# Weight sums made once during the input projection, activation sums on VectorE, and a deeper fetch in a hybrid encoder layer

## The chip, the cores and the metric

The kernel runs on one core of a Trainium2 chip. A core has five engines with a queue of instructions each: TensorE (PE in the profile; its weight loads are PEld), VectorE (DVE), ScalarE (ACT), GpSimd (POOL), and SyncE (SP), which here does nothing but issue transfers. Sixteen DMA engines move data between the chip's main memory and the on-chip buffers. An engine works through its own queue in order and waits where an operand or a buffer is not ready, so one waiting instruction holds up everything behind it on that engine. The metric is the device time of one execution in microseconds (us); lower is better.

## The reference, cut to what matters

One layer is computed for two groups of requests: a prompt of 2048 tokens and 8 x 16 tokens of samples with caches. Both share the weights.

```
h   = RMSNorm(x)
z   = h @ w_in                               # (tokens, 1024) @ (1024, 3592)
A   = chunk-band attention of z's q, k, v    # 8 heads x 64, own chunk + 8 before
B   = mLSTM matrix memory of z's q, k, v, o  # 4 heads x 128
x   = x + RMSNorm(concat(RMSNorm(A), sigmoid(o) * RMSNorm(B)) @ w_out)
u   = RMSNorm(x) @ w_up                      # (tokens, 1024) @ (1024, 5632)
y   = causal depthwise conv of width 3 over u's tokens, plus a bias
gate, up = halves of y's columns
x   = x + RMSNorm((gelu(gate) * up) @ w_down)   # (tokens, 2816) @ (2816, 1024)
```

Everything is float32. The change touches how w_up and w_down, and the activations gelu(gate) * up, are prepared for their two products.

## The kernel before, in words

**Precision.** A float32 matrix is split into a rounded part and the rest (a copy on ScalarE, a subtraction on VectorE: `split`, L1293 to L1295), and each product is made of three matmuls (`mm3`, L97 to L101).

**Two stages.** The first (to about 1340 us) makes the input projection, attention, the mLSTM and the output projection. The loop over `seq` (L1252 onwards) goes through 14 groups of projection columns for each of two halves of the tokens. A group yields after every few matmuls (12 steps for the groups qk and qb; 18 or 16, in the first or second half, for va and vo), and at each step `pump` lets attention and mLSTM work run beside it. Attention work is read back from main memory: the projections are stored there by transfers on ScalarE's queue and loaded by SP's.

The second stage is the feed-forward network, in three blocks of tokens (`FBLOCKS`: 768, 768 and the rest). Each block makes 22 feature tiles of the up-projection and then the down-projection.

**Seven products instead of eight.** The up-projection of every block, and the down-projection of the first two, use a Strassen-type scheme: both matrices are cut into 2 x 2 parts, sums of parts are formed, and 7 products replace 8. This needs

- four sums of the parts of w_up per feature tile. In block 0, `load_quads` (L1299) loads the four parts of a tile (128x512 each), makes the sums on VectorE (L1311), and stores them in main memory (`wsd`, L1313) for the later blocks. Three of the seven operands of the tile are kept on the chip (`raws`) for its second half. Blocks 1 and 2 load all seven from main memory.
- four sums of the parts of w_down per pair of rows. `fold_down` (L1161) makes them in the first stage on GpSimd, from 22 pieces of 512 KB in a buffer tag ("xr") that other work shares, and stores them in `wtd`. Each step of groups 1 to 12 of the first half calls it once.
- four sums of the activations per pair of feature tiles. `store_a` (L1547) stores the plain parts, forms the sums on GpSimd in place (L1559 to L1562), and stores those. Two of the sums overwrite a part that was just handed to a store, and so wait for that store.

**The down-projection** reads these activations back in pieces numbered i, of two feature tiles each: `fetch_a` (L1517) loads a piece, `split_a` (L1532) splits it. Pieces 0 and 1 go to small buffers ("q", 12 of 128x512 floats, which the weights and other work use too); later ones go to row buffers ("yq", 6 of 128x1024 floats), which the convolution's outputs y and g use as well. Pieces 2 and 3 are fetched at the first step of the down loop, later ones four ahead.

**Order.** The engines' orders are laid out when the program is built, by a planner that simulates the time of each instruction and issues what is ready. It can move an instruction ahead of others on its queue; `tc.keep_in_program_order` holds one behind the instruction that the program wrote before it on that queue.

Of the kernel before, what the change touches and what calls it, by code (L numbers as in the profile page):

```python
# [17 lines left out]
P = 128  # L18
D = 1024
# [21 lines left out]
NK = NF // 2  # L41
FORDER = [f for k in range(NK) for f in (k, k + NK)]
# [6 lines left out]
def hymba_step(ctx: ExitStack, tc: tile.TileContext, I: dict, O: dict):  # L49
# [1111 lines left out]
    def fold_down():  # L1161

        for k in range(NK):
            for c in range(2):
                cols = slice(c * 256, (c + 1) * 256)
                t = rows_tile("xr", [P, D], f"fold{k}_{c}").rearrange("p (a n) -> p a n", a=4)
                nc.sync.dma_start(t, I["w_down"][k].rearrange("p (a n) -> p a n", a=4)[:, :, cols])
                yield 0.0, 0.0
                yield 0.0, 0.0
                b11, b12, b22, b21 = [t[:, i] for i in range(4)]  # L1170
                nc.gpsimd.tensor_tensor(b11, b12, b11, op=ALU.subtract)
                nc.gpsimd.tensor_tensor(b12, b22, b12, op=ALU.subtract)
                nc.gpsimd.tensor_tensor(b22, b22, b11, op=ALU.subtract)
                nc.gpsimd.tensor_tensor(b21, b21, b22, op=ALU.subtract)
                yield 0.0, 0.0
                yield 0.0, 0.0
                nc.sync.dma_start(wtd[k].rearrange("p (a n) -> p a n", a=4)[:, :, cols], t)
                yield 0.0, 0.0
# [43 lines left out]
    folds = fold_down()  # L1222
# [5 lines left out]
    for n_, (half, gi) in enumerate(seq):  # L1228
# [68 lines left out]
    raws = {}  # L1297

    def load_quads(b, f, g):  # L1299

        src = lambda i: I["w_up"][f][:, i * 512:(i + 1) * 512]
        if b == 0 and g == 0:
            q = []
            for i in range(4):
                q.append(quad(f"wu{f}_{i}"))
                nc.sync.dma_start(q[i], src(i))
            a11, a12, a22, a21 = q
            s1, s2, s3, s4 = [quad(f"ws{f}_{i}") for i in range(4)]
            for o, x, y, op in ((s1, a21, a22, ALU.add), (s2, s1, a11, ALU.subtract), (s3, a11, a21, ALU.subtract),
                                (s4, a12, s2, ALU.subtract)):  # L1310
                nc.vector.tensor_tensor(o, x, y, op=op)  # L1311
# [12 lines left out]
        return out  # L1324
# [117 lines left out]
    for b, tiles in enumerate(FBLOCKS):  # L1442
# [74 lines left out]
        def fetch_a(i):  # L1517
# [6 lines left out]
            if i < 2:  # L1524
                g[i] = [quad(f"ar{b}_{i}_{x}")[:, :384] for x in range(2)]
                for x, r in enumerate(g[i]):
                    nc.sync.dma_start(r, src[:, 2 * c + x, :])
            else:
                g[i] = row(f"ar{b}_{i}")[:, :n_]
                nc.sync.dma_start(g[i], src[:, ks, :].rearrange("p k n -> p (k n)"))  # L1530
# [16 lines left out]
        def store_a(f, gt):  # L1547
# [11 lines left out]
            nc.gpsimd.tensor_tensor(a11, a11, a21, op=ALU.subtract)  # L1559
            nc.gpsimd.tensor_tensor(a21, a21, a22, op=ALU.add)  # L1560
            nc.gpsimd.tensor_tensor(a22, a22, a11, op=ALU.subtract)
            nc.gpsimd.tensor_tensor(a12, a12, a22, op=ALU.subtract)  # L1562
# [3 lines left out]
        for fi, f in enumerate(FORDER):  # L1566
# [23 lines left out]
            if fi == NF - 1:  # L1590
# [31 lines left out]
        if not last:  # L1622
# [47 lines left out]
            for p, (_, _, set_, onto) in enumerate(SEQUENCE):  # L1670
                for c in range(3):
# [202 lines left out]
```

## Time and profile before

| | us |
|---|---|
| median of 3 runs | 2834.72 |
| lowest and highest | 2833.73, 2836.35 |
| the profiled execution | 2845.43 |
| its span, first to last instruction | 2843.6 |
| TensorE busy in the span | 2707.8 |
| VectorE busy | 1942.6 |
| ScalarE busy | 1442.3 |
| GpSimd busy | 628.5 |

| stretch, us | what runs |
|---|---|
| 0 to 1340 | input projection, attention, mLSTM, output projection |
| 1357 to 1722 | up-projection of block 0 |
| 1711 to about 1870 | down-projection of block 0 |
| 1900 to 2200 | within the up-projection of block 1 |
| 2230 to 2406 | down-projection of block 1 |
| 2406 to 2682 | up-projection of block 2, then its down-projection to the end |

Busy times are of one profiled execution. Matmuls are pipelined and their ends modelled, so a TensorE that is busy all the time can still differ in matmuls per us; a few matmul records may be missing. The granted clock (PEclk) is 1.00 when TensorE may run at full speed. In a row of waits, the first engine and line waited, the second released it. A group's row ends with the idle time of its engine just before the group's instructions, and what ended it.

### The profile page before, as it was taken

To read this page: it belongs to the slowest core of one execution; us is meant where nothing else is said; L and a number is where in the kernel's file an instruction comes from. 1 tells how busy PE (TensorE), PEld (TensorE's weight loads), DVE (VectorE), ACT (ScalarE), POOL (GpSimd) and SP (SyncE) were. 2 spreads that over 40 slices of the span, in tenths; PEclk is the share of its full clock that TensorE was granted. 3 is DMA by queue.
4 is the path that set the end of the run, shared out by engine and by line. 5 is a ranking of instruction groups with operands and counts; after the bars stand their busy time and mean duration, and the time that the engine had idled before them with its cause. 6 is when DMAs were issued, how large, how long until landed. Compare 5 with 4: busy or idle time off the path is not lost. (4 is left out here: it accounts for less than half of the span.)

```text
span 2843.6 us, 47569 instructions
## 1 busy us (share of the span) xinstructions
PE 2707.8 (95%) x16389; PEld 2526.5 (89%) x16389; DVE 1942.6 (68%) x3503; ACT 1442.3 (51%) x2916; POOL 628.5 (22%) x1071
## 2 busy tenths in 40 slices
PE   6889999999899999999999997999999899999998
PEld 6789999988799998878889996889999778999877
DVE  4344445655545668766898997757887785888855
ACT  4244545644445666534444445655554565555543
POOL 3231000111100002244332332112232331122220
PEclk9999999999999999999999999999999999999999
DMA  7775446456564556445655556675555696655585
GB/s 233 205 225 181 130 124 184 153 167 184 167 194 127 157 156 191 126 150 188 222 177 170 173 180 217 217 238 163 175 172 159 235 336 222 195 177 168 182 318 188
DMA packets 359025, 535.12 MB, mean 188 GB/s; under 512 B 58787, under 2 KB 196479, under 8 KB 358655
## 3 DMA queue, kind: packets, MB, share of 16 engines
q1 hardware_dynamic: 318270, 491.95, 55.3%
q10 hardware_dynamic: 38592, 33.83, 3.6%
q0 software_dynamic: 1920, 6.29, 0.6%
q8 instruction: 129, 2.11, 0.3%
q14 instruction: 114, 0.93, 0.1%
HBM read 383.87 MB, written 151.21 MB: 188 GB/s over the span
## 5 line engine op out<-in xcount | busy, mean ns | idle before, releaser
L99 PE MATMUL uec<-B,wuh 128*128 128x384 f32 (+1 forms) x720 | 236.5, 330 | 4.7 <-DVE x L1584 1.8
L100 PE MATMUL uec<-B,wuh 128*128 128x384 f32 (+1 forms) x720 | 235.7, 327 | 0.0
L101 PE MATMUL uec<-B,wul 128*128 128x384 f32 (+1 forms) x720 | 234.5, 327 | 0.0
L1294 ACT CAST wuh<-wu 128x512 fp32r<-128x512 f32 x255 | 141.6, 618 | 80.6 <-PE uec L100 75.5
L1295 DVE TENSOR_TENSOR wul<-wu,wuh 128x512 fp32r<-128x512 f32 x255 | 167.5, 695 | 14.5 <-ACT wuh L1294 10.9
L99 PE MATMUL vo<-wi_h,hT 128*128 128x256 f32 x544 | 155.1, 285 | 0.6 <-DVE mt L206 0.6
L101 PE MATMUL vo<-wi_h,hT 128*128 128x256 f32 x544 | 155.6, 286 | 0.0
L100 PE MATMUL vo<-wi_l,hT 128*128 128x256 f32 x544 | 154.8, 285 | 0.0
L400 DVE CUSTOM_DVE_ANT_0 tmp<-s,nb 128x640 f32<-128x640 f32 (+4 forms) x128 | 94.3, 737 | 84.5 <-PE s L390 83.8
L1295 DVE TENSOR_TENSOR wdl<-wdr,wdh 128x512 fp32r<-128x512 f32 x198 | 130.2, 703 | 28.1 <-ACT wdh L1294 25.7
L99 PE MATMUL dn<-wdh,ah 128*128 128x512 f32 x308 | 123.3, 400 | 22.1 <-ACT ah L1294 21.1
L99 PEld LDWEIGHTS uec<-B,wuh 128*128 128x128 f32 x720 | 135.5, 188 | 9.5 <-DVE x L1584 3.1
L99 PE MATMUL qk<-hT,wi_h 128*128 128x384 f32 (+1 forms) x384 | 130.4, 340 | 7.6 <-ACT qk_st L233 4.6
L100 PEld LDWEIGHTS uec<-B,wuh 128*128 128x128 f32 x720 | 135.7, 188 | 0.2
L101 PEld LDWEIGHTS uec<-B,wul 128*128 128x128 f32 x720 | 135.5, 188 | 0.0
L1294 ACT CAST wdh<-wdr 128x512 fp32r<-128x512 f32 x198 | 111.7, 618 | 46.8 <-DMA wdr<-in_w_down 18.7
L413 DVE TENSOR_TENSOR ptl<-pt,pth 128x640 fp32r<-128x640 f32 (+4 forms) x128 | 93.6, 738 | 59.7 <-ACT pth L412 58.8
L401 ACT ACTIVATE tmp<-tmp,mn 128x640 f32<-128x640 f32 (+4 forms) x128 | 97.5, 762 | 67.5 <-DVE mn L400 61.6
L100 PE MATMUL qk<-hT,wi_h 128*128 128x384 f32 (+1 forms) x384 | 129.2, 337 | 0.0
L101 PE MATMUL qk<-hT,wi_l 128*128 128x384 f32 (+1 forms) x384 | 128.7, 335 | 0.0
L100 PE MATMUL qb<-hT,wi_h 128*128 128x384 f32 (+1 forms) x384 | 127.9, 333 | 0.0
L101 PE MATMUL dn<-wdh,al 128*128 128x512 f32 x308 | 124.5, 404 | 2.8 <-DVE al L1295 2.7
(448 smaller groups left out, 9267.0 us busy)
## 6 DMA issues: line engine op xcount, KB each, us to landing
wu<-in_w_up SPq DMA_DIRECT2D x220, 256.0 KB, 3.9
wu<-wsd SPq DMA_DIRECT2D x176, 256.0 KB, 3.8
wdr<-in_w_down SPq DMA_DIRECT2D x110, 256.0 KB, 5.5
wi_raw<-in_w_in SPq DMA_DIRECT2D x52, 512.0 KB, 4.1
wsd<-ws SPq DMA_DIRECT2D x88, 256.0 KB, 3.5
wdr<-wtd SPq DMA_DIRECT2D x88, 256.0 KB, 6.1
ad_S<-g SPq DMA_DIRECT2D x88, 192.0 KB, 1.8
ar<-ad_S SPq DMA_DIRECT2D x40, 384.0 KB, 6.3
```

The source lines that it names most:

```text
L99: nc.tensor.matmul(out, ah, bh, start=start, stop=False, skip_group_check=onto)
L100: nc.tensor.matmul(out, ah, bl, start=False, stop=False, skip_group_check=onto)
L101: nc.tensor.matmul(out, al, bh, start=False, stop=stop, skip_group_check=onto)
L400: nc.vector.tensor_tensor_reduce(o_, s_, b_, 1.0, 3e38, ALU.add, ALU.min, accum_out=mn)
L401: nc.scalar.activation(tmp[:, :n], tmp[:, :n], AF.Exp, bias=mn, scale=-1.0, accum_out=rsum[:, i % 4, hh:hh + 1])
L413: nc.vector.tensor_tensor(s.ptl[:, sl, qc], ptv, s.pth[:, sl, qc], op=ALU.subtract)
L1294: nc.scalar.copy(h, r)
L1295: nc.vector.tensor_tensor(l, r, h, op=ALU.subtract)
```

## The change

1. `folds` replaces `fold_down`. It goes through 44 pieces of w_up (22 feature tiles, two column halves) and then 22 of w_down. Each piece is 512 KB, loaded to one of three buffers of its own ("fold"), summed in place by four VectorE operations of 128x256, and stored (`wsd` or `wtd`). Loads and stores are held in program order on SP's queue. A piece is begun every 4 steps; its sums are written 3 steps and its store 5 steps after its load. The steps are those of groups 2 to 12 of both halves; what is left is done at the last group.
2. `load_quads` makes no sums any more: block 0 loads seven operands per tile from main memory like the other blocks. The places of the sums within `wsd` change with the order in which they are now made.
3. `store_a` forms the activation sums on VectorE.
4. `fetch_a` uses small buffers for pieces 0 to 4 (before: 0 and 1). Pieces 2 to 4 are fetched while the last feature tile of the block runs, after the splits of pieces 0 and 1; in the down loop the fetch of piece i + 4 begins at i = 1.

```diff
+FOLD_STEPS = 4
...
-    def fold_down():
-        for k in range(NK):
-            for c in range(2):
-                cols = slice(c * 256, (c + 1) * 256)
-                t = rows_tile("xr", [P, D], f"fold{k}_{c}").rearrange("p (a n) -> p a n", a=4)
-                nc.sync.dma_start(t, I["w_down"][k].rearrange("p (a n) -> p a n", a=4)[:, :, cols])
-                yield 0.0, 0.0
-                yield 0.0, 0.0
-                b11, b12, b22, b21 = [t[:, i] for i in range(4)]
-                nc.gpsimd.tensor_tensor(b11, b12, b11, op=ALU.subtract)
...
-                nc.sync.dma_start(wtd[k].rearrange("p (a n) -> p a n", a=4)[:, :, cols], t)
-                yield 0.0, 0.0
+    def fold_pieces():
+        for f in FORDER:
+            for c in range(2):
+                yield f"u{f}_{c}", I["w_up"][f], wsd[f], c, False
+        for k in range(NK):
+            for c in range(2):
+                yield f"d{k}_{c}", I["w_down"][k], wtd[k], c, True
+
+    def folds():
+        v4 = lambda t: t.rearrange("p (a n) -> p a n", a=4)
+        live = deque()
+        pieces = list(fold_pieces())
+
+        def load(nm, src, dst, c, down):
+            cols = slice(c * 256, (c + 1) * 256)
+            t = v4(pr.tile([P, D], F32, tag="fold", name=f"fold{nm}", bufs=3))
+            tc.keep_in_program_order(nc.sync.dma_start(t, v4(src)[:, :, cols]))
+            live.append((t, v4(dst)[:, :, cols], down))
+
+        def combine(t, dst, down):
+            a, b, c, d = [t[:, i] for i in range(4)]
+            sub = lambda o, x, y: nc.vector.tensor_tensor(o, x, y, op=ALU.subtract)
+            if down:
+                sub(a, b, a)
+                sub(b, c, b)
+                sub(c, c, a)
+                sub(d, d, c)
+            else:
+                sub(a, a, d)
+                nc.vector.tensor_tensor(d, d, c, op=ALU.add)
+                sub(c, c, a)
+                sub(b, b, c)
+
+        for n in range(FOLD_STEPS * (len(pieces) + 1)):
+            i, r = divmod(n, FOLD_STEPS)
+            if r == 0 and i < len(pieces):
+                load(*pieces[i])
+            if (n - 3) % FOLD_STEPS == 0 and 0 <= n - 3 < FOLD_STEPS * len(pieces):
+                combine(*live[-1])
+            if (n - 5) % FOLD_STEPS == 0 and 0 <= n - 5 < FOLD_STEPS * len(pieces):
+                t, dst, _ = live.popleft()
+                tc.keep_in_program_order(nc.sync.dma_start(dst, t))
+            yield
...
-            if half == 0 and 1 <= gi <= 12:
-                next(folds, None)
+            if 2 <= gi <= 12:
+                next(fold, None)
...
+        if n_ == len(seq) - 1:
+            for _ in fold:
+                pass
...
     def load_quads(b, f, g):
-        if b == 0 and g == 0:
-            q = []
-            for i in range(4):
-                q.append(quad(f"wu{f}_{i}"))
-                nc.sync.dma_start(q[i], src(i))
-            a11, a12, a22, a21 = q
-            s1, s2, s3, s4 = [quad(f"ws{f}_{i}") for i in range(4)]
-            for o, x, y, op in ((s1, a21, a22, ALU.add), (s2, s1, a11, ALU.subtract), (s3, a11, a21, ALU.subtract),
-                                (s4, a12, s2, ALU.subtract)):
-                nc.vector.tensor_tensor(o, x, y, op=op)
-            for i, o in enumerate((s2, s3, s1, s4)):
-                nc.sync.dma_start(wsd[f][:, i * 512:(i + 1) * 512], o)
-            raws[f] = [a12, a22, s4]
-            return [a11, s2, s3, s1]
-        if b == 0:
-            return raws.pop(f)
-        for i, s_ in enumerate([[src(0), kept(0), kept(1), kept(2)], [src(1), src(2), kept(3)]][g]):
+        for i, s_ in enumerate([[src(0), kept(2), kept(0), kept(3)], [src(1), src(2), kept(1)]][g]):
...
-            if i < 2:
+            if i < 5:
                 g[i] = [quad(f"ar{b}_{i}_{x}")[:, :384] for x in range(2)]
...
-            nc.gpsimd.tensor_tensor(a11, a11, a21, op=ALU.subtract)
+            nc.vector.tensor_tensor(a11, a11, a21, op=ALU.subtract)
...
                 else:
                     split_a(0)
                     split_a(1)
+                    for i in range(2, 5):
+                        fetch_a(i)
...
                         if k % 2 == 0:
-                            if i == 0:
-                                fetch_a(2)
-                                fetch_a(3)
                             if i >= 1:
                                 split_a(i + 1)
-                            fetch_a(i + 4)
+                                fetch_a(i + 4)
```

More of the change, by code (lines that the diff above doesn't have):

```diff
@@ L1159, in late_B @@
             nc.vector.tensor_tensor(lo, lo.bitcast(F32), hi, op=ALU.subtract)
-    def fold_down():
+    def fold_pieces():
+        for f in FORDER:
+            for c in range(2):
+                yield f"u{f}_{c}", I["w_up"][f], wsd[f], c, False
         for k in range(NK):
             for c in range(2):
-                cols = slice(c * 256, (c + 1) * 256)
-                t = rows_tile("xr", [P, D], f"fold{k}_{c}").rearrange("p (a n) -> p a n", a=4)
-                nc.sync.dma_start(t, I["w_down"][k].rearrange("p (a n) -> p a n", a=4)[:, :, cols])
-                yield 0.0, 0.0
-                yield 0.0, 0.0
-                b11, b12, b22, b21 = [t[:, i] for i in range(4)]
-                nc.gpsimd.tensor_tensor(b11, b12, b11, op=ALU.subtract)
-                nc.gpsimd.tensor_tensor(b12, b22, b12, op=ALU.subtract)
-                nc.gpsimd.tensor_tensor(b22, b22, b11, op=ALU.subtract)
-                nc.gpsimd.tensor_tensor(b21, b21, b22, op=ALU.subtract)
-                yield 0.0, 0.0
-                yield 0.0, 0.0
-                nc.sync.dma_start(wtd[k].rearrange("p (a n) -> p a n", a=4)[:, :, cols], t)
-                yield 0.0, 0.0
+                yield f"d{k}_{c}", I["w_down"][k], wtd[k], c, True
@@ L1221, in hymba_step @@
     next(norms)
-    folds = fold_down()
+    fold = folds()
     pend = load_group(0)
@@ L1558, in store_a @@
             a11, a21, a12, a22 = gt1[:, 0:384], gt1[:, 384:768], first, second
[L1559 to L1562, printed above, removed]
+            nc.vector.tensor_tensor(a11, a11, a21, op=ALU.subtract)
+            nc.vector.tensor_tensor(a21, a21, a22, op=ALU.add)
+            nc.vector.tensor_tensor(a22, a22, a11, op=ALU.subtract)
+            nc.vector.tensor_tensor(a12, a12, a22, op=ALU.subtract)
             for what, src in (("S3", a11), ("S1", a21), ("S2", a22), ("S4", a12)):
```

1 line of the change is left out of this document (removed).

## The prediction

> **What bounds the kernel now.** First the page: TensorE is the bound on average, VectorE is next, and VectorE is not spread evenly.
>
> ```profile
> span 2843.6 us, 47569 instructions
> PE 2707.8 (95%) x16389; PEld 2526.5 (89%) x16389; DVE 1942.6 (68%) x3503; ACT 1442.3 (51%) x2916; POOL 628.5 (22%) x1071
> ```
> ```profile
> PE   6889999999899999999999997999999899999998
> DVE  4344445655545668766898997757887785888855
> ```
>
> The first fence is busy time, share and instruction count of each engine; the second cuts the span in 40 slices, each digit a busy share in tenths. TensorE idles 136 us in all. To see where, I read busy times by stretch: start and end, length, then the busy us and instruction count of each engine, the granted TensorE clock, the DMA engines' share and GB/s.
>
> ```profile
> core 0: us, PE busy (x) PEld busy (x) DVE busy (x) ACT busy (x) POOL busy (x), PEclk, DMA share, GB/s
> 0.00:108.00 108.00, 80.28 (x503) 75.36 (x503) 48.65 (x115) 37.92 (x70) 37.12 (x73) 0.93 0.78 226
> 108.00:250.00 142.00, 125.92 (x808) 123.50 (x807) 54.80 (x113) 57.03 (x133) 42.82 (x59) 0.94 0.72 215
> 150.00:250.00 100.00, 93.10 (x621) 91.92 (x622) 44.71 (x91) 45.48 (x104) 35.13 (x48) 0.97 0.72 219
> 250.00:480.00 230.00, 227.35 (x1649) 223.01 (x1649) 115.48 (x273) 117.97 (x284) 11.30 (x38) 1.00 0.48 145
> 250.00:1340.00 1090.00, 1062.13 (x7320) 999.40 (x7320) 655.08 (x1459) 572.93 (x1393) 175.08 (x371) 1.00 0.52 158
> 1400.00:1700.00 300.00, 282.27 (x1573) 273.68 (x1572) 277.48 (x391) 140.68 (x228) 95.48 (x112) 0.99 0.54 176
> 1900.00:2200.00 300.00, 300.00 (x1722) 299.87 (x1721) 238.27 (x341) 153.31 (x251) 81.94 (x121) 1.00 0.58 177
> 2400.00:2660.00 260.00, 260.00 (x1763) 258.99 (x1761) 221.72 (x449) 148.82 (x261) 56.93 (x166) 1.00 0.58 179
> 1741.00:1870.00 129.00, 127.00 (x565) 102.98 (x564) 89.48 (x129) 79.80 (x140) 11.99 (x14) 0.99 0.72 230
> 1730.00:1740.00 10.00, 1.70 (x4) 1.38 (x5) 5.16 (x7) 4.17 (x6) 1.79 (x4) 0.50 0.66 220
> ```
>
> Four places lose time. (1) 0 to 250: 44 us idle with the DMA at 0.72 to 0.78. (2) 250 to 1340: 28 us idle in 1090, VectorE 60% busy. (3) The up-projection of block 0 (1400 to 1700): 1573 matmuls in 300 us, where the same code in block 1 (1900 to 2200) does 1722. Block 0 has VectorE at 92%, block 1 at 79%. (4) The turn from up- to down-projection (1730 to 1740; part 3 shows a second one).
>
> **Change, part 1: block 0 loses its weight sums.**
>
> ```profile
> L1311 DVE TENSOR_TENSOR ws<-wu,wu 128x512 f32<-128x512 f32 x36 | 24.7, 685 | 17.5 <-DMA wu<-in_w_up 15.9 <-DMA wsd<-ws 1.6
> L1311 DVE TENSOR_TENSOR ws<-ws,wu 128x512 f32<-128x512 f32 x18 | 13.9, 773 | 0.0
> L1311 DVE TENSOR_TENSOR ws<-wu,ws 128x512 f32<-128x512 f32 x18 | 12.2, 680 | 0.0
> L1458 DVE TENSOR_TENSOR uu<-x,uec 128x384 f32<-128x384 f32 x19 | 10.3, 544 | 0.3 <-PE uec L101 0.3
> ```
> ```profile
> PE uec L99 <- DVE x L1584: 13.2, 9, 3.3
> ```
>
> The first three rows (groups of VectorE instructions in 1400 to 1700: count, busy us, mean ns, idle us before them; 18 feature tiles) are 50.8 us of VectorE, and 17.5 us more were idle before them. The last fence, a row of the waits in 1340 to 1710, shows TensorE waiting there for VectorE to empty an accumulator. Part 2 brings 4 sums per pair of tiles: 9 pairs x 4 x 0.544 = 19.6 us. So VectorE's work for this stretch becomes 277.5 - 50.8 + 19.6 = 246.3 us. At block 1's rate the stretch takes 300 x 1573/1722 = 274 us, so VectorE would be 90% busy. The third block runs TensorE at 100% with VectorE at 221.7/260 = 85%, so 90% is a little beyond what is shown to be harmless. The whole block has 22 x 7 x 12 = 1848 matmuls: 352.4 us at the first rate, 321.9 at the second. Ends: -30.5, if it runs as block 1, and -17, if the 13.2 us of waits stay because VectorE is still at 90%. I take **-27**, nearer the first, as 85% costs nothing and 92% costs all of it. DMA: the 4 stores per tile go, and 7 tiles are loaded instead of 4, which is block 1's traffic (share 0.58, TensorE 100%), so I charge nothing.
>
> **Part 2: activation sums from GpSimd to VectorE, both of the first two blocks.**
>
> ```profile
> L1559 POOL TENSOR_TENSOR g<-g 128x384 f32<-128x384 f32 x22 | 26.1, 1187 | 97.8 <-DMA ad_A<-g 73.4 <-DVE y L1479 12.1 <-DVE ws L1311 7.7
> ```
> ```profile
> 1978.28 1.01 DVE L1478 SCALAR_TENSOR_TENSOR y<-uu,wcv,y 128x768 f32<-128x768 f32 x1
> 1979.33 1.65 DVE L1479 SCALAR_TENSOR_TENSOR y<-uu,wcv,y 128x768 f32<-128x768 f32 x1
> ```
> ```profile
> 1975.50 0.80 SPq L1548 DMA_DIRECT2D ad_A<-g  x2
> ```
> ```profile
> 1978.47 1.69 POOL L1561 TENSOR_TENSOR g<-g,g 128x384 f32<-128x384 f32 x1 [1.90 <-DMA ad_A<-g]
> ```
>
> Four operations like the first row's leave GpSimd per pair (four lines, 22 of each, 1.19 us this one); VectorE gets 4 x 0.544 = 2.2 us, in all 88 x 0.544 = 48 us. In block 1: 238.3 + 10 pairs x 2.2 = 260 of 300 us, 87%. Two of the four overwrite a tile whose store was just issued: the store at 1975.50 released the sum at 1978.47, 3.0 us later. On GpSimd that wait held up only a few two-column copies; on VectorE it holds whatever is queued behind, and those are the evacuations that TensorE waits for. The upper end is 44 waits x 3.0 = 132 us of VectorE; the lower is nothing, if the order puts other work between. The nearest row is VectorE's own wait for a load, 15.9 us over 18 tiles, 0.88 us each: 44 x 0.88 = 39 us, inside the free 10% and 13% of two blocks of 322 us (74 us). I charge **+2** for both blocks. Something comes back: the y operation beside GpSimd's sum took 1.65 us, its twin 1.01.
>
> The Trainium skill (GPSIMD Engine Reference, 1. Specifications) says GpSimd shares its SBUF interfaces with VectorE, contending with VectorE's two-input instructions. By that rule part 2 costs less than 2.2 us a pair and my 90% would be nearer 88%, which would put part 1 at its -30.5; the 1.65 us agrees, but one coincidence doesn't give a total.
>
> **Part 3: more activations fetched ahead (i < 5, and the fetches pulled before the down loop).**
>
> ```profile
> 1738.30 0.80 PE L99 MATMUL dn<-wdh,ah 128*128 128x512 f32 x1 [11.04 <-ACT ah L1294]
> ```
> ```profile
> 1732.55 0.91 SPq L1530 DMA_DIRECT2D ar<-ad_A  x2
> ```
> ```profile
> 1729.21 1.89 DVE L1295 TENSOR_TENSOR wdl<-wdr,wdh 128x512 fp32r<-128x512 f32 x3
> ...
> 1732.93 0.96 DVE L1609 TENSOR_TENSOR g<-y,y 128x768 f32<-128x768 f32 x1 [0.91 <-ACT y L1481]
> ```
> ```profile
> PE dn L99 <- ACT ah L1294: 10.0, 1, 10.0
> ```
>
> Pieces 0 and 1 wait in small buffers; piece 2 needs a row buffer that the last y tiles hold until about 1733, so its load goes out at 1732.55 and TensorE waits 11.0 us, and 10.0 us at the second turn. Afterwards pieces 2 to 4 are there too: 3 x 18 matmuls at 127.00/565 = 0.225 us (1741 to 1870) = 12 us of work. What is late next: the weight splits, whose last ends at 1731.1, and piece 5, which still needs a row at 1733. I leave 3 us of wait at each turn. The loads take 6 more of 12 small buffers that the weights also use. Ends: -24 (both waits, and 3 us more for the granted clock of 0.50 in 1730 to 1740) and 0 (weights wait for buffers). I take **-16**.
>
> **Part 4: 66 weight pieces in the input projection.** Before, 22 pieces on GpSimd, early; after, 66 on VectorE, one per four steps.
>
> ```profile
> core 0: us, POOL busy (x), PEclk, DMA share, GB/s
> 0.00:108.00 108.00, 28.06 (x36) 0.93 0.78 226
> 108.00:250.00 142.00, 41.29 (x52) 0.94 0.72 215
> 150.00:250.00 100.00, 34.68 (x44) 0.97 0.72 219
> ```
> ```profile
> L363 DVE TENSOR_TENSOR vhl<-vraw,vhl 128x256 fp32r<-128x256 f32 x40 | 17.3, 432 | 30.1 <-ACT vhl L362 30.1
> ```
> ```profile
> 108.00:480.00 372.00, 22.82 (x40) 0.98 0.57 171
> 600.00:950.00 350.00, 21.71 (x38) 1.00 0.57 168
> ```
> ```profile
> 126.75 0.48 ACT L231 COPY qk_st<-qk 128x384 f32<-128x384 f32 x1 [9.52 <-DMA qTd<-qk_st]
> ```
> ```profile
> 127.28 0.44 PE L99 MATMUL qk<-hT,wi_h 128*128 128x384 f32 x1 [2.95 <-ACT qk_st L231]
> ```
>
> The first fence counts GpSimd's sums, four to a piece: 9 pieces before 108, 13 in 108 to 250, 11 of them after 150. The third counts the casts of the projection weights (L1201, four to a group), which place the groups: about ten groups in 108 to 480, nine and a half in 600 to 950. The new generator runs in groups 2 to 12 of both halves: 7 x 12 + 4 x 18 = 156 steps, 39 pieces, from about 105 to 500 (10 us a piece), and 27 pieces from about 602 to 920. So nothing before 108 (9 fewer), as many as now up to 250, and 25 + 27 = 52 where there were none. VectorE: 264 x 0.432 = 114 us, of which 52 x 1.73 = 90 us fall after 250: 655 + 90 of 1090 us, 68%.
>
> Gain before 108: 27.7 us are idle, some 10 of them the start; half of the rest, **-9**. Cost after 250: each piece moves 1 MB (SP issues 132 transfers for them instead of 44) and brings four sums, both tied to SP's queue, where a store that waits for its sums holds every load behind it. Price by rows: in 150 to 250, 6.9 us idle with 11 pieces, 0.63 us a piece; in 108 to 250, 16.1 with 13, 1.24 a piece. The last two fences show how it goes: a projection's store, competing with them, kept ACT 9.5 us and TensorE 2.95. Below zero it can't go, as nothing leaves this stretch. I take half of 0.63, since the sums are now shorter than GpSimd's and have buffers of their own, while the idle time in 150 to 250 has other causes too: 52 x 0.31 = **+16**.
>
> **Sum.** -27 + 2 - 16 - 9 + 16 = -34 us. The span 2843.6 becomes 2810. The profiled run (2845.43 us) is 0.4% above the median of the three runs, 2834.72, so against that median: 2801 us.
>
> **Rivals.**
> *Pieces cost what they cost early* (slower). At 1.24 us each: 52 x 1.24 = 64, less 9, plus -41 for the rest = +14: 2849. For it: 52 MB come on top of 1090 us at 0.52, and in 250 to 480 (0.48 now) 1 MB per 10 us is some 100 GB/s more, which by the row's 145 GB/s at 0.48 makes 0.8, above what 108 to 250 has. Against: in 1741 to 1870 TensorE is 98% busy with the DMA at 0.72, and the sums no longer run beside VectorE on GpSimd. It decides from 50/52 = 0.96 us a piece.
> The Trainium skill (DMA: Bandwidth & Descriptors, Queues, rings and completion order) says a semaphore increment lands only after every earlier write of that DMA engine, across its queues. By it each new 0.5 MB store delays other loads' completion, which speaks for this rival; the 9.52 us wait agrees.
> *VectorE sits in the waits for stores* (slower). 132 us less the 74 free: +58 instead of +2: 2857. It decides from 1.7 us a wait.
> *The turns stay*: weights wait for small buffers; -18 in all: 2817.
> *Nothing is lost in the projection*: part 1 -30, turns -22, part 4 -12: -64: 2771.
>
> **How the numbers follow.** Forecast 0.42, pieces cost 0.20, stores 0.06, turns stay 0.12, nothing lost 0.20. About 0.2% (6 us) is what can be told from no change. Faster: 0.42 + 0.20 + most of 0.12 less some tail: 0.71; slower 0.20 + 0.06 less a little: 0.24; same 0.05. The range reaches from under the best case to the first rival: 2760 to 2850.
>
> **What would show it.** Block 0 at 5.7 matmuls per us, VectorE near 90%, no L1311. TensorE's wait for ah at the two turns from 11 and 10 to about 3. GpSimd without sums; VectorE's sums in 384 columns idle under 1 us before them for a DMA. In 250 to 950 TensorE idle up by some 16 us, the DMA share at 0.7. Wrong if that stretch loses over 50 us, or block 0 stays under 5.5 per us.

## The result, and the profile after

The changed kernel takes 2806.44 us in the median (2802.77 to 2808.13); the kernel before, beside it, 2835.34 (2833.73 to 2836.35). The ratio is 0.9897, 95% interval [0.988, 0.9914]: 29 us faster, where 34 were forecast. The profiled execution of the changed kernel took 2806.19 us, close to its median. That of the kernel before took 2845.43, 10 us above its own. So the two profiles differ by 39 us, and 10 of these are not the change's.

The page of the changed kernel: span, busy time of each engine, and the 40 slices.

```profile
span 2804.4 us, 47643 instructions
PE 2709.0 (97%) x16389; PEld 2527.3 (90%) x16389; DVE 1985.5 (71%) x3773; ACT 1439.9 (51%) x2922; POOL 441.3 (16%) x895
...
PE   8899999989999999999999999999999999999998
...
DVE  5355566656666767766788888668888875888855
```

GpSimd lost its sums (628.5 to 441.3 us), VectorE does 43 us more, and TensorE idles 95 us instead of 136. VectorE's row is flatter: the slices at 9 are gone from block 0, and the first stage's 4s and 5s became 5s and 6s. The stretches of the changed kernel (columns as in the prediction):

```profile
core 0: us, PE busy (x) PEld busy (x) DVE busy (x) ACT busy (x) POOL busy (x), PEclk, DMA share, GB/s
0.00:108.00 108.00, 89.17 (x561) 84.86 (x562) 53.61 (x137) 41.96 (x79) 10.21 (x37) 0.97 0.63 196
108.00:250.00 142.00, 138.36 (x932) 135.52 (x932) 74.26 (x171) 66.18 (x154) 2.13 (x7) 1.00 0.61 188
250.00:600.00 350.00, 335.45 (x2445) 326.14 (x2444) 217.70 (x545) 173.62 (x418) 30.08 (x99) 0.99 0.69 217
600.00:930.00 330.00, 310.19 (x2123) 292.23 (x2122) 204.15 (x530) 149.09 (x366) 32.66 (x102) 0.98 0.79 246
930.00:1340.00 410.00, 396.37 (x2521) 354.59 (x2520) 286.27 (x565) 231.82 (x570) 103.08 (x163) 1.00 0.51 163
1400.00:1700.00 300.00, 299.42 (x1702) 296.41 (x1700) 253.64 (x388) 151.72 (x246) 40.48 (x81) 1.00 0.54 172
1900.00:2200.00 300.00, 299.45 (x1698) 296.04 (x1698) 256.92 (x393) 156.42 (x257) 37.77 (x84) 1.00 0.54 171
1741.00:1870.00 129.00, 127.78 (x572) 105.18 (x571) 87.82 (x130) 78.66 (x144) 18.75 (x21) 1.00 0.68 225
```

Block 0 (1400 to 1700) now runs as block 1, at 5.67 matmuls per us with VectorE at 85%. TensorE's waits for VectorE to empty an accumulator, 13.2 us in 1340 to 1710 before, are gone from that window (who waited, who released; us in total, times, longest):

```profile
PE dn L100 <- ACT wdh L1325: 1.9, 2, 1.4
PE ua L102 <- DVE wul L1326: 0.4, 1, 0.4
```

Before 250 TensorE gained 8.9 and 12.4 us. After 250 it lost 20: 48 us idle in 250 to 1340, against 28.

TensorE's waits at the two turns of the changed kernel, in the same columns, first 1700 to 1800, then 2175 to 2340:

```profile
PE dn L100 <- ACT wdh L1325: 1.4, 1, 1.4
PE dn L101 <- DVE wdl L1326: 1.4, 1, 1.4
PE dn L102 <- DVE al L1326: 1.2, 1, 1.2
```
```profile
PE dn L100 <- ACT wdh L1325: 3.5, 4, 1.6
PE dn L102 <- DVE al L1326: 2.6, 3, 1.5
PE dn L101 <- DVE wdl L1326: 2.2, 3, 1.4
```

The wait for ah is gone from both. At the second turn many small waits for splits of weights and activations took part of its place.

For the experiments I cut the profiles at the matmuls that begin and end each part: first matmul of block 0's up-projection, last matmul into its last accumulators, first of block 1, and so on. The time up to the first of these is called the first stage. These are cuts of single profiles. The first stage is 1345.4, 1349.8 and 1351.5 us in the three kernels below that run the old first stage in exactly the old order of instructions, so the 1357.2 of the profile before is on the long side.

| us | first stage | block 0 up | turn, down 0 | block 1 up | turn, down 1 | rest |
|---|---|---|---|---|---|---|
| before | 1357.2 | 364.4 | 177.5 | 330.9 | 174.2 | 439.4 |
| after | 1367.5 | 330.6 | 163.6 | 331.0 | 172.0 | 439.7 |
| forecast | +7 | -26 | turns: -16 | +1 | | 0 |
| measured | +10.3 | -33.8 | -13.9 | +0.1 | -2.2 | +0.3 |

### The profile page after: what moved, and what is told of

Its sections match the earlier page's. It is cut to its first block, busy times and chain, and to the rows that moved or that the text cites. A ratio compares the mean times of both kernels' runs of the same rounds, so it can differ in the third digit from the quotient of the medians.

```text
span 2804.4 us, 47643 instructions
## 1 busy us (share of the span) xinstructions
PE 2709.0 (97%) x16389; PEld 2527.3 (90%) x16389; DVE 1985.5 (71%) x3773; ACT 1439.9 (51%) x2922; POOL 441.3 (16%) x895
## 4 chain that ended last, share of the span: by engine, by line
PE 51%; DVE 2%; DMA 2%; ACT 1%; issue 1%; POOL 1%; SPq 0%; DVEq 0%; POOLq 0%; ACTq 0%
PE uec L100 6%; PE uec L101 6%; PE uec L102 6%; PE ua L102 3%; PE ua L101 3%; PE ua L100 3%; PE dn L101 3%; PE dn L102 3%; PE dn L100 3%; PE dnm L101 2%; PE dnm L100 2%; PE dnm L102 2%; PE ub L100 2%; PE ub L101 2%; PE ub L102 2%; PE wo L102 1%
## 5 line engine op out<-in xcount | busy, mean ns | idle before, releaser
L1326 DVE TENSOR_TENSOR wul<-wu,wuh 128x512 fp32r<-128x512 f32 x315 | 202.9, 686 | 14.9 <-ACT wuh L1325 12.1
L1325 ACT CAST wuh<-wu 128x512 fp32r<-128x512 f32 x315 | 172.9, 618 | 72.4 <-PE uec L101 68.7
L1325 ACT CAST wu<-wu 128x512 fp32r<-128x512 f32 x147 | 85.0, 617 | 87.6 <-PE uec L101 61.6
L102 PE MATMUL qb<-hT,wi_l 128*128 128x384 f32 (+1 forms) x384 | 127.9, 333 | 0.0
```

Of the source, the lines that this page charges most:

```text
L102: nc.tensor.matmul(out, al, bh, start=False, stop=stop, skip_group_check=onto)
L1325: nc.scalar.copy(h, r)
L1326: nc.vector.tensor_tensor(l, r, h, op=ALU.subtract)
```

## The experiments

### One part alone, and two together

*Parts 1 and 4 alone*: the changed kernel with activation sums on GpSimd and the old fetch.

```diff
-            nc.vector.tensor_tensor(a11, a11, a21, op=ALU.subtract)
+            nc.gpsimd.tensor_tensor(a11, a11, a21, op=ALU.subtract)
...
-            if i < 5:
+            if i < 2:
                 g[i] = [quad(f"ar{b}_{i}_{x}")[:, :384] for x in range(2)]
...
```

> The change with parts 2 and 3 undone: activation sums on GpSimd again, two pieces fetched ahead. Theory (the parts act in their own stages): the first stage as in the changed kernel (+10 us), the up-projection of block 0 shorter by 25 to 34 us since VectorE loses 51 us of sums per 300 us there, both turns with their 11 and 10 us waits: about 2815 us. Rival (block 0 needs the sums off GpSimd too): block 0 gains 12 us at most, about 2833 us.

*Part 2 alone*: the kernel before, with the four sums of `store_a` on VectorE.

> The kernel before with only the activation sums moved to VectorE. Theory (VectorE is the bound of block 0): VectorE goes from 92% to about 97% there, block 0 is 5 to 10 us longer, block 1 (79% to 87%) unchanged: about 2842 us. Rival (GpSimd's sums slow VectorE by contention by as much as they take): no change or up to 5 us faster. Rival (VectorE sits in waits for stores): 20 us or more slower, with waits for ad_A before its 384-column sums of 1 us or more each.

*Part 3 alone*: the kernel before, with the new fetch.

> The kernel before with only the deeper fetch. Theory (the turn waits for a row buffer): the 11 us wait of the first turn goes, and some 12 to 14 us with it; the second turn gains about 2 us as in the changed kernel, where its one wait became many small ones: about 2820 us. Rival (the second turn was spoilt by the other parts): 10 us from it too, about 2812 us. Rival (small buffers run short): under 5 us in all.

*Parts 2 and 3*: the kernel before with both, and with its own weight sums.

> The kernel before with the deeper fetch and the activation sums on VectorE, its weight sums unchanged (in block 0, and 22 pieces on GpSimd). Alone these two gave -20 and -6 us. Theory (they add up, and the 66 pieces give back in the first stage what block 0 gains): about -26, 2807 us, which is the time of the whole change. Rival (VectorE in block 0 gets too full with both, and the weight part earns its 34 us): 2820 us or more.

| | median, us | ratio to before | first stage | block 0 up | turn, down 0 | turn, down 1 |
|---|---|---|---|---|---|---|
| parts 1, 4 | 2820.97 | 0.9958 [0.9944, 0.9972] | 1361.0 | 330.0 | 175.6 | 175.9 |
| part 2 | 2826.78 | 0.998 [0.9967, 0.9992] | 1349.8 | 356.3 | 180.4 | 174.9 |
| part 3 | 2812.5 | 0.9928 [0.9913, 0.9944] | 1345.4 | 361.8 | 163.0 | 169.6 |
| parts 2, 3 | 2809.51 | 0.9895 [0.9882, 0.9908] | 1351.5 | 356.1 | 161.3 | 168.3 |

Each median has runs of the kernel before beside it, from 2832.82 to 2838.72 in the tables of this document, so small differences are better read from the ratios. Each part gains alone: 12, 6 and 20 us, 38 together, where the whole change has 29. Parts 2 and 3 without any change to the weight sums are as fast as the whole (0.9895 and 0.9897). So on top of them parts 1 and 4 are worth nothing: block 0 gives 25.5 us (356.1 to 330.6), and the first stage takes 16 back (1351.5 to 1367.5), with the turns taking 6 more. Part 3 alone has its gain where the prediction put it, 14.5 us at the first turn and 4.6 at the second; that its total came out as the first rival's 2812 is chance, as that rival expected 10 us from the second turn.

Part 1 by itself brings block 0 fully to block 1's pace, whatever the other parts do. Part 2 by itself gains 8 us in the same block (5.5 against the 361.8 of part 3 alone, where that code is the old one), and the groups of VectorE show why. First the kernel before, then part 2 alone, both in 1400 to 1700 (count, busy us, mean ns, idle before):

```profile
L1479 DVE SCALAR_TENSOR_TENSOR y<-uu,wcv,y 128x768 f32<-128x768 f32 x19 | 23.3, 1226 | 0.1
L1478 DVE SCALAR_TENSOR_TENSOR y<-uu,wcv,y 128x768 f32<-128x768 f32 x19 | 22.4, 1181 | 2.3 <-ACT y L1477 2.3
L1295 DVE TENSOR_TENSOR wul<-ws,wuh 128x512 fp32r<-128x512 f32 x52 | 41.8, 823 | 0.0
```
```profile
L1478 DVE SCALAR_TENSOR_TENSOR y<-uu,wcv,y 128x768 f32<-128x768 f32 x19 | 19.3, 1014 | 1.5 <-ACT y L1477 1.5
L1479 DVE SCALAR_TENSOR_TENSOR y<-uu,wcv,y 128x768 f32<-128x768 f32 x19 | 19.2, 1013 | 0.0
L1295 DVE TENSOR_TENSOR wul<-ws,wuh 128x512 fp32r<-128x512 f32 x49 | 32.8, 685 | 0.0
...
L1561 DVE TENSOR_TENSOR g<-g,g 128x384 f32<-128x384 f32 x10 | 5.5, 553 | 2.3 <-DMA ad_A<-g 2.3
L1559 DVE TENSOR_TENSOR g<-g 128x384 f32<-128x384 f32 x9 | 5.0, 551 | 0.0
```

The y operations fall from a mean of 1.2 to 1.01 us, 7 us over the 38 shown, and the subtractions of the weight splits (L1295) fall too. By start and end times in the trace of the kernel before, the 26 of 75 y operations in 1400 to 1700 that overlap one of GpSimd's four sums take 1.32 us in the mean, the others 1.01; the 23 of 133 splits that overlap one take 1.26 us, the other 110 take 0.68 and none of these over 0.70. That is some 21 us of VectorE's time, 13 of it in the splits. The additions that read an accumulator (L1458) are not slowed: 0.55 us where they overlap a sum, 0.54 elsewhere. So the four sums, at 0.55 us each, cost VectorE about what it gets back: it does 21.5 us of added sums at 279.84 us busy against 277.48, with 1603 matmuls done in place of 1573. The waits for stores in front of the sums are small. The loss that was expected (about 2842) did not come; the rival that names contention with GpSimd did. The Trainium skill (GPSIMD Engine Reference, 1. Specifications) says the two engines share SBUF interfaces; these rows agree.

### What the 66 pieces cost

*No pieces*: the generator is never called, and the second stage reads plain parts in place of sums, with the same traffic there.

```diff
-            if 2 <= gi <= 12:
-                next(fold, None)
...
-        kept = lambda i: wsd[f][:, i * 512:(i + 1) * 512]
+        kept = src
...
-            src = I["w_down"][k] if blk < 4 else wtd[k]
+            src = I["w_down"][k]
```

> The changed kernel without the 66 pieces: no loads, sums or stores of them, and the products read the plain parts in place of the sums, so the sums of w_up and w_down are left out. Theory (each piece costs TensorE time after 250 us): 25 to 40 us faster than the changed kernel, about 2775 us, all of it before 1368 us. Rival (the pieces are hidden and the first stage's 10 us come from another order of its work): within 8 us of the changed kernel.

It took 2758.38 us, 0.9736 [0.9721, 0.9751]. That is 48 us under the change (46 by the two ratios), more than the 25 to 40 expected, and the profiles have 45 of it in the first stage (1322.2 against 1367.5). So a piece costs about 48/66 = 0.73 us, with whatever the planner's other order without pieces is worth. The kernel before is not free of this: in the three kernels that keep its first stage's code, its 22 pieces make that stage 1345 to 1352 us, some 23 to 29 above 1322, which is over 1 us for each of the 22.

Which part of a piece costs it? Three kernels look at the sums. *No sums* drops the four operations and keeps loads and stores; *sums tied* holds the first sum of a piece in program order on VectorE; *pieces on GpSimd* makes the sums there.

```diff
-                combine(*live[-1])
+                pass
```

> The changed kernel with the pieces loaded and stored but not summed (the sums of w_up and w_down are left out). Without the pieces altogether the time was 2758 us, with them 2806: 48 us to be shared out. Theory A (VectorE: 112 us of sums and 88 us in which VectorE stood waiting for the pieces' loads): at least 30 of the 48 us go, 2776 us or less. Theory B (the DMA traffic of 66 MB and SP's queue): at most 15 us go, 2791 us or more.

```diff
+            tie = tc.keep_in_program_order
...
-                sub(a, b, a)
+                tie(sub(a, b, a))
...
-                sub(a, a, d)
+                tie(sub(a, a, d))
```

> The changed kernel with the first sum of each piece held in program order on VectorE's queue, 3 steps behind the piece's load. Theory A1 (the waits of 88 us are the cost, as the planner places the sums when it thinks the load has landed): VectorE's waits for pieces fall under 25 us and the time by 10 to 25 us, 2781 to 2796 us. Theory A2 (the work of the sums is the cost) or B (DMA): the waits fall and the time stays within 5 us of 2806.

```diff
-            sub = lambda o, x, y: nc.vector.tensor_tensor(o, x, y, op=ALU.subtract)
+            sub = lambda o, x, y: nc.gpsimd.tensor_tensor(o, x, y, op=ALU.subtract)
...
-                nc.vector.tensor_tensor(d, d, c, op=ALU.add)
+                nc.gpsimd.tensor_tensor(d, d, c, op=ALU.add)
```

> The changed kernel with the pieces' sums on GpSimd (about 0.74 us each in place of 0.42), all else the same. Theory A: VectorE is rid of work and waits, GpSimd waits instead and nothing of weight is queued behind it: 15 to 35 us faster than 2806 us. Theory B (DMA): within 8 us of 2806. Theory C (GpSimd's sums slow VectorE's two-input operations beside them, and SP waits longer for its stores): slower than 2806 us.

| | median, us | ratio to before | first stage |
|---|---|---|---|
| after | 2806.44 | 0.9897 [0.988, 0.9914] | 1367.5 |
| no sums | 2794.17 | 0.9858 [0.9839, 0.9876] | 1358.7 |
| sums tied | 2810.93 | 0.9911 [0.9895, 0.9927] | 1372.2 |
| pieces on GpSimd | 2809.93 | 0.9907 [0.9891, 0.9923] | 1377.7 |
| no pieces | 2758.38 | 0.9736 [0.9721, 0.9751] | 1322.2 |

My theory had been that VectorE stands in front of pieces that haven't landed. The waits exist: VectorE's in the first stage of the changed kernel, and then with the sums tied:

```profile
DVE foldu L1185 <- DMA foldu<-in_w_up: 67.9, 34, 8.2
...
DVE foldd L1185 <- DMA foldd<-in_w_down: 20.5, 15, 3.5
```
```profile
DVE foldu L1186 <- DMA foldu<-in_w_up: 27.6, 13, 4.8
DVE foldd L1186 <- DMA foldd<-in_w_down: 14.6, 11, 3.0
```

By the bounds set before, the theory fell. 88 us of waits became 42 (under 25 was expected) and nothing was gained; without any sums, and so without the waits and without 112 us of VectorE's work, only 12 us came back. With the sums on GpSimd, VectorE is rid of the same work and waits, and the time is the change's within the intervals; but there 17 of 104 splits of projection weights (L1230) overlap GpSimd's sums and take 0.95 us instead of 0.69, so this run alone would not decide. (Its profile is 8 us above its median, so its 1377.7 is on the long side.) The other 36 us of the 48 go with the loads and stores: their traffic, their places on SP's queue, or the order into which the planner lays everything else around them. That order is another one in each of these kernels, so 12 and 36 are differences of whole programs and no clean prices.

### Where the pieces run, and in what order

*Untied*: loads and stores free to move. *Stores free*: loads tied, stores free. *Wide*: untied, and whole tiles of 1 MB in 33 pieces, one begun every 8 steps, with one buffer of twice the size in place of three.

```diff
-            tc.keep_in_program_order(nc.sync.dma_start(t, v4(src)[:, :, cols]))
+            nc.sync.dma_start(t, v4(src)[:, :, cols])
...
-                tc.keep_in_program_order(nc.sync.dma_start(dst, t))
+                nc.sync.dma_start(dst, t)
```

> The changed kernel with the pieces' loads and stores free on SP's queue. Theory (the planner takes loads forward to where their buffers are free): the pieces start before 50 us, crowd the first 250 us as in the kernel before, and the first stage is 10 to 30 us longer: 2816 to 2836 us. Rival (the order matters little, three buffers already limit how early a piece can come): within 6 us of 2806.

```diff
             tc.keep_in_program_order(nc.sync.dma_start(t, v4(src)[:, :, cols]))
...
-                tc.keep_in_program_order(nc.sync.dma_start(dst, t))
+                nc.sync.dma_start(dst, t)
```

> The changed kernel with the pieces' loads still held in program order on SP's queue and their stores free. The version with both free took 2792.3 us, 0.9848 of the kernel before; the change 0.9897. Theory S (a store that waits for its sums holds every load behind it, the mechanism the prediction named): freeing the stores brings the whole of the 14 us, 2790 to 2796, ratio 0.984 to 0.986, with the loads still spread over 68 to 959 us. Theory L (what helps is that the loads run early, before 400 us, and leave the stretch from 600 on alone): with the loads still tied the pieces keep their places, the first stage stays near 1367 us and the time at 2802 to 2809, ratio 0.989 to 0.991.

```diff
-            t = v4(pr.tile([P, D], F32, tag="fold", name=f"fold{nm}", bufs=3))
-            tc.keep_in_program_order(nc.sync.dma_start(t, v4(src)[:, :, cols]))
+            t = v4(pr.tile([P, 2 * D], F32, tag="fold", name=f"fold{nm}", bufs=1))
+            nc.sync.dma_start(t, v4(src))
...
```

> The changed kernel with untied pieces of a whole tile: 33 pieces of 1 MB, one buffer of 128x2048 in place of three of 128x1024, 8 KB in a row per partition in place of 1 KB. Theory (the DMA engines' time is the cost, and short rows make it longer): DMA share per GB/s falls in the stretch with pieces, and the time by 8 to 20 us against the untied 2792: 2772 to 2784 us. Rival (the bytes alone cost): 2786 to 2798 us. Rival (one buffer: a piece waits for its predecessor's store, and the planner's order suffers): slower than 2800 us.

| | median, us | ratio to before | first stage | pieces run, us |
|---|---|---|---|---|
| untied | 2792.32 | 0.9848 [0.9831, 0.9865] | 1359.9 | 9 to 399 |
| after | 2806.44 | 0.9897 [0.988, 0.9914] | 1367.5 | 68 to 959 |
| stores free | 2819.96 | 0.9928 [0.9908, 0.9948] | 1388.0 | 68 to 962 |
| wide | 2834.81 | 0.9981 [0.9967, 0.9994] | 1402.7 | 8 to 588 |

Untied was expected to be slower, and it is the fastest kernel of the study that computes the whole layer: 14 us under the change, 44 under the kernel before that ran beside it (2835.91). Its stretches, then those of the kernel without pieces, then those with stores free:

```profile
0.00:108.00 108.00, 85.84 (x527) 80.90 (x528) 69.06 (x180) 38.18 (x69) 13.17 (x37) 0.94 0.91 298
108.00:250.00 142.00, 132.81 (x882) 128.95 (x880) 91.19 (x223) 65.80 (x157) 2.30 (x7) 0.99 0.97 298
250.00:600.00 350.00, 332.94 (x2429) 323.13 (x2429) 219.00 (x534) 176.43 (x420) 32.07 (x92) 0.99 0.73 225
600.00:930.00 330.00, 316.13 (x2203) 300.40 (x2204) 177.28 (x468) 155.93 (x384) 33.65 (x109) 0.99 0.55 166
930.00:1340.00 410.00, 403.00 (x2579) 363.17 (x2578) 287.46 (x549) 233.26 (x566) 106.69 (x168) 1.00 0.50 158
```
```profile
0.00:108.00 108.00, 90.11 (x571) 86.54 (x571) 49.48 (x125) 41.81 (x78) 10.25 (x37) 0.98 0.56 176
108.00:250.00 142.00, 139.67 (x941) 138.52 (x942) 64.02 (x138) 70.99 (x163) 2.25 (x7) 0.99 0.41 124
250.00:600.00 350.00, 342.04 (x2518) 334.43 (x2517) 188.29 (x468) 178.60 (x434) 36.14 (x107) 0.99 0.49 150
600.00:930.00 330.00, 321.54 (x2277) 308.01 (x2276) 183.00 (x465) 166.93 (x411) 33.76 (x107) 0.99 0.55 169
```
```profile
600.00:930.00 330.00, 307.89 (x2113) 291.00 (x2112) 200.47 (x527) 145.45 (x361) 32.14 (x97) 0.98 0.81 251
930.00:1340.00 410.00, 385.71 (x2434) 344.04 (x2434) 273.72 (x552) 224.22 (x555) 91.84 (x153) 0.98 0.50 153
```

The planner, let loose, pulls all pieces before 400 us, 38 of the 66 before 250 where the change has 13, and the DMA engines stand at 0.91 and 0.97. That costs TensorE 9 us before 250 against the changed kernel and 2.5 in 250 to 600; from 600 on it has 13 us back. By 1340 the busy times are level, and untied has done 8620 matmuls against 8582. So more than half of the pieces pushed into the start, at a DMA share near 1, cost less, in this pair, than the same traffic spread at 0.6 to 0.8.

But this is no rule that early is good. Wide is early too, and 42 us slower than untied (38 by the ratios). The rival "one buffer" came there: up to 600 us SP waited 51.7 us, in 15 waits, for the store that had to free the buffer before the next load. The longer rows saved little: up to 600 us the DMA share per GB/s was 2 to 8% under untied's. Stores free has the pieces where the change has them, and its first stage was 20 us longer, half of that lost in 930 to 1340: 11 us of TensorE's time less than the change, though pieces run only in the first 32 us of that stretch, as in the change. Both theories missed: freeing the stores gave neither the 14 us nor the old time.

Nor did it take away SP's waits for sums. These are SP's waits before the pieces' stores (L1205) for sums on VectorE, in 0 to 1000, in the changed kernel and then with stores free:

```profile
SPq L1205 <- DVE foldd L1185: 7.2, 4, 5.2
SPq L1205 <- DVE foldu L1185: 4.6, 3, 2.3
```
```profile
SPq L1205 <- DVE foldu L1185: 24.6, 18, 2.9
SPq L1205 <- DVE foldd L1185: 14.5, 8, 4.0
```

12 us became 39, as the stores moved nearer to their sums (the first one goes out at 77.8 us instead of 89.6). Untied has 27 us of these waits and is the fastest, so they don't settle the time by themselves either.

What every edit to the pieces changes is the order. By the traces, leaving out the pieces' own instructions, VectorE's order up to 1340 us is the change's for the first 112 instructions with stores free, for 13 untied and for 7 in wide, out of some 1680; the three kernels with parts 2 and 3 alone or together keep the old order throughout. That the order laid out for attention and mLSTM is itself worth ten us and more fits the 11 us lost in 930 to 1340, where hardly a piece runs, but no run changes the order and nothing else. So this part of the 36 us can't be told from the traffic's, and the share of each stays open.

### The second turn

The finishing transfers of block 0's rows (normed outputs read, added, stored) fall into the up-projection and turn of block 1. This kernel leaves those rows of block 0 out.

```diff
-        done = [u for t, rs in unfinished for u in later(t, rs)]
+        done = [u for t, rs in unfinished for u in later(t, rs)] if last else []
```

> The changed kernel without the finishing of block 0's output rows beside block 1's down-projection (the y rows of block 0 are left out: 24 loads, 12 additions and stores less of that kind). Theory (the second turn gained only 2 to 5 us where the first gained 14, because these transfers fill the DMA engines there and weights arrive late): the stretch from the last up matmul to the next block's first falls from 172 to about 163 us, and ACT's casts wdh are no longer what TensorE waits for. Rival (small buffers run short in both turns alike): it stays at 169 us or more.

One execution took 2798.38 us: turn and down-projection of block 1 159.8 us against 172.0, and block 0's unchanged (163.2). The stretches of the change and of this kernel at the second turn:

```profile
2180.00:2230.00 50.00, 45.55 (x202) 36.29 (x201) 43.60 (x64) 32.79 (x57) 9.29 (x16) 0.97 0.78 270
2230.00:2280.00 50.00, 45.75 (x199) 35.62 (x198) 40.48 (x56) 30.85 (x58) 23.30 (x22) 0.97 0.90 310
```
```profile
2180.00:2230.00 50.00, 48.98 (x234) 40.98 (x233) 43.92 (x66) 34.05 (x60) 4.59 (x13) 1.00 0.76 251
2230.00:2280.00 50.00, 49.94 (x229) 39.48 (x228) 40.45 (x65) 37.04 (x72) 6.08 (x8) 1.00 0.77 254
```

So most of what stands at the second turn, once the wait for ah is gone, goes with the finishing work of the block before: DMA share 0.90 there, 0.77 without it, and TensorE's waits for splits 1 us instead of 8. This is one execution, and it doesn't tell the transfers from the additions. These run on GpSimd in the changed kernel, and the weight splits on VectorE get longer beside them (2180 to 2280; the change's additions and splits, then the splits of the quiet turn):

```profile
L1429 POOL TENSOR_TENSOR f<-f,x 128x512 f32<-128x512 f32 x9 | 19.9, 2207 | 27.6 <-DVE f L1428 24.9 <-DMA ad_A<-g 2.7
L1326 DVE TENSOR_TENSOR wdl<-wdr,wdh 128x512 fp32r<-128x512 f32 x41 | 29.3, 751 | 1.3 <-ACT wdh L1325 1.3
```
```profile
L1326 DVE TENSOR_TENSOR wdl<-wdr,wdh 128x512 fp32r<-128x512 f32 x44 | 28.1, 685 | 1.7 <-ACT wdh L1325 1.7
```

The 11 splits that overlap an addition take 0.93 us, the other 30 take 0.69.

## Why the prediction was right, and where it was off

**Direction and size.** -34 forecast, -29 measured by the medians; 2801 forecast, 2806 measured. The largest gain and the largest loss were named, with their places. That the sum comes so near is partly luck: the terms were off by more than it. And the working had parts 1 and 4 bring 20 of the 34 and parts 2 and 3 bring 14, while parts 2 and 3 without the others have the whole gain (0.9895 against 0.9897): on top of them the new weight sums, the largest part of the change, bring nothing.

**Part 1** (-27, ends -30.5 and -17). Block 0 up became 33.8 us shorter, 34.4 with parts 2 and 3 undone (31 against the 361.8 of part 3 alone). The end "runs as block 1" held; the 13.2 us of waits for VectorE did not stay. The choice between the ends failed because VectorE came to 85%, not 90%: with GpSimd's sums gone, the y operations and the weight splits got shorter. The working noted this for the y operations and gave it no price; the splits, the larger share, it did not see. The limit itself was read rightly: 85% costs nothing.

**Part 2** (+2; ends 0 and 132 us of VectorE's waits). It gains: 6 us alone, so the sign of this term was wrong. The waits for stores were over-sized: of 44 such sums the 21 in 1400 to 1700 idled 12 us.

```profile
L1572 DVE TENSOR_TENSOR g<-g 128x384 f32<-128x384 f32 x11 | 6.1, 558 | 7.3 <-DMA ad_A<-g 7.2
L1574 DVE TENSOR_TENSOR g<-g,g 128x384 f32<-128x384 f32 x10 | 5.6, 555 | 5.0 <-DMA ad_A<-g 5.0
```

That is 0.6 us a wait, against 0.88 taken and 3.0 at the far end. The rival "VectorE sits in the waits for stores" is out. (Its 1.7 us a wait is only where the 74 us free on VectorE are used up; by the working's own terms the forecast gain of 34 would be used up at 2.5.) The step that failed is "something comes back", put into the sum at nothing: the relief of VectorE's operations beside GpSimd's sums was some 21 us in 300 us of block 0, as much as the moved sums cost there. Once part 1 has emptied VectorE it brings nothing more in block 0 (330.0 without it, 330.6 with it).

**Part 3** (-16, ends -24 and 0, 3 us left at each turn). Alone -20; in the change 13.9 + 2.2 = 16 by the stages. The total is right and its halves are not, which is luck: the working's 8 and 7 us, with something for the clock, came as 13.9 and 2.2. At the first turn the three rows shown are 4 us of waits, near the 3 left; but smaller waits of 2.6, 2.0 and 0.5 us that stood beside the 11.0 before were not counted. At the second the question "what is late next" was answered too kindly: 8.3 us of small waits stay, and by the quiet turn most of them go with the finishing work of the block before, which the working did not name. The rival "the turns stay" is out.

**Part 4** (-9, 0, +16). Before 108 us TensorE gained 8.9: as forecast, though six pieces left that stretch and not nine. In 108 to 250 it gained 12.4 where nothing was forecast. The sums of w_up on line 1185, three to a piece, place the pieces of the changed kernel:

```profile
0.00:108.00 108.00, 3.78 (x9) 0.97 0.63 196
108.00:250.00 142.00, 12.24 (x29) 1.00 0.61 188
```

Three pieces run before 108, where none were expected, and some ten in 108 to 250 in place of 13. A quarter fewer, and yet three quarters of the 16 us idle there went; so that idle time was not the price of pieces as such. After 250 the loss was 20 us by TensorE's busy time, forecast 16. The stage as a whole is 10 us longer by the two profiles, forecast 7; but the profile of before is some 10 us long, and against the kernels that share its first stage (1345 to 1352) the change's loss there is 16 to 22.

The step that failed is the price, read off the idle time beside the old pieces. "Half of 0.63" was a little small in its own stretch, 20 us over the 53 pieces after 250, or 0.38 us each. But against the kernel without pieces the runs give 0.73 us for each of the 66, and the 22 old pieces, which the working took as costing only what is idle before 250, had cost some 25 us over the whole stage. So the stage lost 16 to 22 us where +7 was forecast. That stays below the 41 us that the other parts were to bring, so the first rival is out and the change still wins. The mechanism named, a store on SP's queue that waits for its sums and holds loads, is neither shown nor excluded: SP's waits of that kind are 12 us in the changed kernel, and the run that was to take them away has 39. The Trainium skill (DMA: Bandwidth & Descriptors, Queues, rings and completion order), cited for that rival, speaks of completions held back by earlier writes; untied, with DMA at 0.97 and 298 GB/s, is the fastest, so these runs give the rule no visible price here, nor do they exclude one.

**What would make it wrong** (250 to 950 losing over 50 us; block 0 under 5.5 matmuls per us) did not come.

## What to carry to other kernels

Price moved background work by leaving it out altogether, not by the idle time around it: here the change's pieces cost 0.73 us each, the kernel before already paid more than 1 us for each of its 22, and the gain in block 0 was nearly all paid back in the stage that took the work over. Before a full engine is given more work, see which of its operations overlap the engine that is to lose it: here they gave back as much as was added. When two edits relieve the same engine in the same stage, don't add their gains. Where a planner lays out the order, test its freedom as an edit of its own: dropping two ties was worth 14 us, dropping one of them was worth nothing or worse.

## What the runs showed that I had not expected

- VectorE's y operation on 128x768 takes 1.01 us alone and 1.32 in the mean where it overlaps one of GpSimd's sums on 128x384, a weight split on 128x512 0.68 and 1.26, so taking GpSimd's sums over made block 0 faster, not slower.
- A stretch of 142 us with the DMA engines at 0.97 of their time (298 GB/s) left TensorE 94% busy (132.81 us), 5.6 us below the change at 0.61; in 600 to 930 the change at 0.79 was 5.9 us below untied at 0.55. The DMA share alone doesn't tell what a stage loses.
- Halving the 88 us of VectorE's waits for pieces changed no time that could be measured, though the order changed with it.
- Three kernels with the same first-stage code, run in the same order of instructions, had 1361.0, 1367.5 and 1372.6 us there in their profiles (parts 1 and 4 alone, the change, the quiet turn). A first stage that differs by 10 us between two single profiles needs the medians beside it.
